# Instance normalisation of 65,536 rows: a direct emission of the program, and tiles whose rows are shared out in sixteen runs

## The chip, the cores and the metric

The kernel runs on one core of a Trainium2 chip. The metric is the device time of one execution in microseconds; lower is better. Several runs of the same program are taken, and their median is compared. A profile is one further execution, recorded by the hardware profiler.

## The reference

```python
def setup_inputs():
    batch = 256
    channels = 256
    length = 4096
    return {
        "x": np.random.randn(batch, channels, length).astype(np.float32),
        "eps": np.float32(1e-5),
    }

def reference(x, eps):
    mean = np.mean(x, axis=2, keepdims=True)
    var = np.var(x, axis=2, keepdims=True)
    return ((x - mean) / np.sqrt(var + eps)).astype(np.float32)
```

Each of the 256 x 256 = 65,536 rows of 4096 fp32 numbers is normalised by its own mean and variance. Rows do not depend on one another, so the order in which they are taken is free, as long as a result goes back to the place that its row came from. Input and output are 1.07 GB each, and every byte crosses the core once in each direction.

## The kernel before, in words

The rows are cut into 128 tiles of 512 rows. A tile lies in SBUF as 128 partitions (P) times K = 4 rows times 4096 numbers: 64 KB in a partition, 8 MB in all. In HBM a tile is one contiguous piece of 8 MB, and partition p holds the four rows that start at 64 KB times p. There are three tile buffers, `X[0]` to `X[2]` (BUFS = 3), and tile t uses buffer t mod 3.

Every wait is written out by hand with semaphores. The helper `take` waits for a count and clears the semaphore (L67 and L68). Four engines have work:

- SP issues every DMA. `load` (L170) waits until the buffer's last store has landed and then loads a tile; `store` (L165) waits until the tile's results are complete and writes it back. In the steady loop SP alternates: store tile t, then load tile t + 2 into the buffer that tile t - 1 left. `store_half` (L181) and two half loads (L199) handle the first and the last tile in halves, so that less lies bare at both ends.
- VectorE, in `vector_tile`, multiplies each row by 1/d and sums it in the same pass to get the mean (L87), forms the reciprocal of the deviation and the bias (L98, L100), and applies scale and bias to three and a quarter of the four rows (L112).
- ScalarE, in `scalar_tile`, squares and sums each row about its mean (L137), takes the square root (L146), and normalises the first 3072 numbers of the fourth row (L151).
- `rows_of` gives the piece of HBM for a tile. For a tile inside the loop the tile number comes from the loop's register.

The loop has 41 rounds of three tiles, tiles 2 to 124. Tiles 0 and 1 come ahead of it, and 125 to 127 after it. The program of each engine is written in a function of its own inside an `nc.Block()`.

A transfer of a tile is one DMA of 128 partitions. Sixteen DMA engines carry it out together, and each adds one to the transfer's semaphore when its share is through, so the wait is for 16.

Of the kernel before, what the change touches and what calls it, by code (L numbers as in the profile page):

```python
# [10 lines left out]
def kernel(  # L11
# [6 lines left out]
    nc = tc.nc  # L18
# [4 lines left out]
    P = 128  # L23
    K = 4
    BUFS = 3
    Q = 3072

    x_flat = x.flatten_outer_dims()
    out_flat = out.flatten_outer_dims()
    n, d = x_flat.shape  # L30
    assert n % (P * K) == 0 and d & (d - 1) == 0

    ntiles = n // (P * K)
    x_t = x_flat.rearrange("(t p k) d -> t p k d", p=P, k=K)
    out_t = out_flat.rearrange("(t p k) d -> t p k d", p=P, k=K)
    assert ntiles == 128

    half = K // 2

# [4 lines left out]
    eps_tile = pool.tile([P, 1], fp32)  # L44

    junk = psum.tile([P, d], fp32)
    X = [pool.tile([P, K, d], fp32, name=f"x{s}") for s in range(BUFS)]
# [8 lines left out]
    loaded = [nc.alloc_semaphore(f"loaded{s}") for s in range(BUFS + 1)]  # L56
    stored = [nc.alloc_semaphore(f"stored{s}") for s in range(BUFS + 1)]
# [6 lines left out]
    ready = nc.alloc_semaphore("ready")  # L64

    def take(engine, sem, count):
        engine.wait_ge(sem, count)  # L67
        engine.sem_clear(sem)  # L68

    V, A, S = nc.vector, nc.scalar, nc.sync  # L70

    def vector_tile(s, r0=0, k=K, ld=None, dn=None):

        x = X[s]
        ld = loaded[s] if ld is None else ld
        dn = done[s] if dn is None else dn
        own = 0

        def mine(instruction):
            nonlocal own  # L80
            own += 1
            return instruction.then_inc(own_v, 1)

        if ld:
            take(V, ld, 16)
        for r in range(r0, r0 + k):
            V.tensor_scalar(  # L87
                out=x[:, r, :], in0=x[:, r, :], scalar1=1.0 / d, scalar2=None, op0=ALU.mult, op1=ALU.add,
                accum_out=mean[s][:, r : r + 1],
            ).then_inc(means, 1)  # L90
        for b in range(r0, r0 + k, 2):
            c = slice(b, b + 2)
            final = b == r0 + k - 2
            if final:
                take(V, stds, (b - r0) // 2 + 1)
            else:
                V.wait_ge(stds, (b - r0) // 2 + 1)
            mine(V.reciprocal(out=rstd[s][:, c], in_=std[s][:, c]))  # L98
            V.wait_ge(own_v, own)
            mine(V.scalar_tensor_tensor(  # L100
                out=nbias[s][:, c], in0=mean[s][:, c], scalar=-1.0 / d, in1=rstd[s][:, c], op0=ALU.mult, op1=ALU.mult
            ))
            if final:
                take(V, own_v, own)
            else:
                V.wait_ge(own_v, own)
            if final:
                V.sem_inc(scaled, 1)
            for r in range(b, b + 2):
                c = slice(r, r + 1)  # L110
                f = slice(Q, d) if r == r0 + k - 1 else slice(0, d)
                V.tensor_scalar(  # L112
                    out=x[:, r, f], in0=x[:, r, f], scalar1=rstd[s][:, c], scalar2=nbias[s][:, c],
                    op0=ALU.mult, op1=ALU.add,
                ).then_inc(dn, 1)

    def scalar_tile(s, r0=0, k=K, ld=None, dn=None):

        x = X[s]
        dn = done[s] if dn is None else dn  # L120
        last = r0 + k - 1
        own = 0

        def mine(instruction):
            nonlocal own
            own += 1
            return instruction.then_inc(own_a, 1)

        for r in range(r0, last + 1):
            c = slice(r, r + 1)  # L130
            if own:
                A.wait_ge(own_a, own)
            if r == last:
                take(A, means, k)
            else:
                A.wait_ge(means, r - r0 + 1)
            mine(A.activation(  # L137
                out=junk, in_=x[:, r, :], func=AF.Square, bias=mean[s][:, c], scale=-float(d), accum_out=ss[s][:, c]
            ))
            if (r - r0) % 2:  # L140
                c = slice(r - 1, r + 1)
                if r == last:
                    take(A, own_a, own)
                else:
                    A.wait_ge(own_a, own)
                A.activation(  # L146
                    out=std[s][:, c], in_=ss[s][:, c], func=AF.Sqrt, bias=eps_tile, scale=1.0 / d**3
                ).then_inc(stds, 1)
        c = slice(last, last + 1)
        take(A, scaled, 1)  # L150
        A.activation(  # L151
            out=x[:, last, :Q], in_=x[:, last, :Q], func=AF.Identity, bias=nbias[s][:, c], scale=rstd[s][:, c]
        ).then_inc(dn, 1)

    def rows_of(ap, t):

        if isinstance(t, int):
            return ap[t]
        first, period, count, i = t
        ap = ap[first : first + period * (count - 1) + 1 : period]  # L160
        return ap[bass.ds(i, 1)].rearrange("o p k d -> p (o k) d")

    def store(s, t):
        take(S, done[s], K + 1)
        S.dma_start(out=rows_of(out_t, t), in_=X[s][:, :, :]).then_inc(stored[s], 16)  # L165

    def load(s, t, wait=True):
        if wait:
            take(S, stored[s], 16)
        S.dma_start(out=X[s][:, :, :], in_=rows_of(x_t, t)).then_inc(loaded[s], 16)  # L170

    def half_of(h):
        return slice(h * half, (h + 1) * half)

    def second(sems, s, h):
        return sems[BUFS] if h else sems[s]

    def store_half(s, t, h):
        r = half_of(h)
        take(S, second(done, s, h), half + 1)  # L180
        S.dma_start(out=out_t[t][:, r, :], in_=X[s][:, r, :]).then_inc(second(stored, s, h), 16)  # L181

    def halves(tile_fn, s, first):
        for h in range(2):
            ld = second(loaded, s, h) if first or h == 0 else False
            tile_fn(s, h * half, half, ld, second(done, s, h))

    last = ntiles - 1
    rounds = (ntiles - 5) // BUFS
    L0 = 2  # L190

    with tc.tile_critical():  # L192
        with nc.Block() as block:  # L193

            @block.sync
            def _(sync):
                for h in range(2):
                    r = half_of(h)
                    S.dma_start(out=X[0][:, r, :], in_=x_t[0][:, r, :]).then_inc(second(loaded, 0, h), 16)  # L199
                load(1, 1, wait=False)  # L200
                store_half(0, 0, 0)
                store_half(0, 0, 1)
                load(2, 2, wait=False)
                store(1, 1)
                take(S, stored[BUFS], 16)
                load(0, 3)

                with S.Fori(0, rounds) as i:
                    for t in range(L0, L0 + BUFS):
                        store(t % BUFS, (t, BUFS, rounds, i))  # L210
                        load((t + 2) % BUFS, (t + 2, BUFS, rounds, i))
                load(last % BUFS, last)
                store((last - 2) % BUFS, last - 2)
                store((last - 1) % BUFS, last - 1)
                store_half(last % BUFS, last, 0)
                store_half(last % BUFS, last, 1)
                for s in ((last - 2) % BUFS, (last - 1) % BUFS, last % BUFS, BUFS):
                    take(S, stored[s], 16)

            @block.vector  # L220
            def _(vector):
                V.memset(eps_tile, eps / d**2).then_inc(ready, 1)  # L222
                halves(vector_tile, 0, True)
                vector_tile(1)
                with V.Fori(0, rounds) as i:  # L225
                    for j in range(BUFS):
                        vector_tile((L0 + j) % BUFS)
                vector_tile((last - 2) % BUFS)
                vector_tile((last - 1) % BUFS)
                halves(vector_tile, last % BUFS, False)  # L230

            @block.scalar
            def _(scalar):
                take(A, ready, 1)
                halves(scalar_tile, 0, True)
                scalar_tile(1)
                with A.Fori(0, rounds) as i:
                    for j in range(BUFS):
                        scalar_tile((L0 + j) % BUFS)
                scalar_tile((last - 2) % BUFS)  # L240
                scalar_tile((last - 1) % BUFS)
                halves(scalar_tile, last % BUFS, False)


# [33 lines left out]
```

## Time and profile before

| What | Value |
|---|---|
| median of 9 runs | 4962.34 us (4961.73 to 4964.0) |
| the profiled execution, its own time | 4962.7 us |
| its span, first to last instruction | 4960.9 us |
| HBM read, written | 1073.74 MB each, 433 GB/s over the span |
| VectorE, ScalarE busy | 3297.8 us, 2407.6 us |
| transfers | 129 loads, 130 stores |
| a load or a store, time for SP to issue it (median) | 0.35 us, 0.34 us |
| from issue to landing (median) | loads 50.3 us, stores 31.5 us |

The times of one execution hang together as follows: the span is what the trace covers, and the execution's own time is some 2 us longer. The page's line of GB/s gives, for 40 equal slices of the span, what the core's DMA engines moved in both directions together. The time from issue to landing is long because a transfer queues behind those issued before it.

### The profile page before, as it was taken

The page shows a single profiled execution, that of the slowest core. Times are in us where ns is not written, and L with a number is a line of the kernel's source. Part 1 is how long each engine was busy: PE and PEld are TensorE (multiplying, and loading weights), DVE is VectorE, ACT ScalarE, POOL GpSimd, SP SyncE. Part 2 cuts the span into 40 slices and gives each one's busy share as a digit, 9 for nine tenths or more (in the row PEclk, how much of TensorE's full clock was granted, in tenths as well). Part 3 has the DMA queues.
Part 4 walks back from the last instruction along what each step waited for, and adds up shares of the span by engine and source line. Part 5 has one row for each costly group of instructions (what it writes and reads, how often), then busy time and mean ns, then how long its engine had stood idle before and what let it go on. Part 6 is the DMA issues. An engine that isn't in the chain of part 4 may idle for free.

```text
span 4960.9 us, 5954 instructions
## 1 busy us (share of the span) xinstructions
DVE 3297.8 (66%) x2049; ACT 2407.6 (49%) x1412; POOL 0.2 (0%) x4
## 2 busy tenths in 40 slices
DVE  6666666666666666666666666666666666666666
ACT  4445444554445544455445544455444554445544
POOL 0000000000000000000000000000000000000000
DMA  9999999999999999999999999999999999999999
GB/s 423 431 431 434 434 432 434 435 432 434 435 433 434 434 435 434 433 435 435 432 434 436 432 435 434 435 433 434 435 433 434 434 435 432 434 435 433 434 435 403
DMA packets 37298, 2147.52 MB, mean 433 GB/s; under 512 B 4144, under 2 KB 4144, under 8 KB 4144
## 3 DMA queue, kind: packets, MB, share of 16 engines
q1 hardware_dynamic: 37296, 2147.50, 100.0%
q14 instruction: 2, 0.02, 0.0%
HBM read 1073.74 MB, written 1073.74 MB: 433 GB/s over the span
## 4 chain that ended last, share of the span: by engine, by line
DVE 62%; another core or an unknown queue 31%; issue 4%; DMA 2%; ACT 0%; DVEq 0%; ACTq 0%; SPq 0%
DVE x L87 44%; DVE x L112 16%; DMA x<-in_x_dram 1%; DVE nbias L100 1%; DMA out_dram<-x 1%; DVE rstd L98 1%; ACT junk L137 0%; DVEq L68 0%; DVEq L225 0%; ACT L146 0%; ACT std L146 0%; DVEq L193 0%; ACTq L68 0%; ACTq L67 0%
## 5 line engine op out<-in xcount | busy, mean ns | idle before, releaser
L87 DVE TENSOR_SCALAR_CACHE_REDUCE x<-x 128x4096 f32<-128x4096 f32 x512 | 2232.3, 4416 | 1581.0 <-DMA x<-in_x_dram 1581.0
L137 ACT ACTIVATE junk<-x,mean 128x4096 f32<-128x4096 f32 x512 | 1883.1, 3678 | 2367.8 <-DVE x L87 2367.8
L112 DVE TENSOR_SCALAR x<-x,rstd,nbias 128x4096 f32<-128x4096 f32 (+1 forms) x512 | 1004.1, 2003 | 33.9 <-DVE nbias L100 29.2
L151 ACT ACTIVATE x<-x,nbias,rstd 128x3072 f32<-128x3072 f32 x130 | 383.2, 2947 | 146.0 <-DVEq L68 146.0
L137 ACT ACTIVATION_READ_ACCUMULATOR junk<-x,mean 128x1 f32 x512 | 95.5, 186 | 0.0
L146 ACT ACTIVATE std<-ss,eps_tile 128x2 f32<-128x2 f32 x256 | 75.6, 295 | 19.1
L98 DVE RECIPROCAL rstd<-std 128x2 f32<-128x2 f32 x256 | 40.6, 158 | 19.4 <-ACT std L146 19.4
L100 DVE SCALAR_TENSOR_TENSOR nbias<-mean,rstd 128x2 f32<-128x2 f32 x256 | 41.1, 160 | 8.9
L87 DVE DVE_READ_ACCUMULATOR x<-x 128x1 f32 x512 | 42.3, 83 | 0.0
L137 ACT ACT_TABLE_LOAD x1 | 1.3, 1283 | 1.2 <-DVE eps_tile L222 1.2
L146 ACT ACT_TABLE_LOAD x1 | 1.3, 1283 | 0.1
L222 DVE MEMSET eps_tile<- 128x1 f32 x1 | 0.1, 59 | 1.0 <-SPq L192 1.0
L259 POOL MEMSET const-uint8-127<- 128x1 uint8 x1 | 0.1, 102 | 0.0
L259 POOL MEMSET const-bfloat16-1.0<- 128x1 bf16 x1 | 0.1, 101 | 0.0
L259 POOL MEMSET const-float32-0.0<- 128x1 f32 x1 | 0.1, 98 | 0.2 <-issue 0.2
L259 POOL MEMSET const-float32-1.0<- 128x1 f32 x1 | 0.1, 98 | 0.0
## 6 DMA issues: line engine op xcount, KB each, us to landing
out_dram<-x SPq DMA_DIRECT2D x4, 4096.0 KB, 19.5
x<-in_x_dram SPq DMA_DIRECT2D x2, 4096.0 KB, 16.8
x<-in_x_dram SPq DMA_DIRECT2D x127, 50.3
out_dram<-x SPq DMA_DIRECT2D x126, 31.5
```

The costliest lines, as they stand in the source:

```text
L87: V.tensor_scalar(out=x[:, r, :], in0=x[:, r, :], scalar1=1.0 / d, scalar2=None, op0=ALU.mult, op1=ALU.add, accum_out=mean[s][:, r : r + 1 ...
L98: mine(V.reciprocal(out=rstd[s][:, c], in_=std[s][:, c]))
L100: mine(V.scalar_tensor_tensor(out=nbias[s][:, c], in0=mean[s][:, c], scalar=-1.0 / d, in1=rstd[s][:, c], op0=ALU.mult, op1=ALU.mult))
L112: V.tensor_scalar(out=x[:, r, f], in0=x[:, r, f], scalar1=rstd[s][:, c], scalar2=nbias[s][:, c], op0=ALU.mult, op1=ALU.add,).then_inc(dn, 1)
L137: mine(A.activation(out=junk, in_=x[:, r, :], func=AF.Square, bias=mean[s][:, c], scale=-float(d), accum_out=ss[s][:, c]))
L146: A.activation(out=std[s][:, c], in_=ss[s][:, c], func=AF.Sqrt, bias=eps_tile, scale=1.0 / d**3).then_inc(stds, 1)
L151: A.activation(out=x[:, last, :Q], in_=x[:, last, :Q], func=AF.Identity, bias=nbias[s][:, c], scale=rstd[s][:, c]).then_inc(dn, 1)
L222: V.memset(eps_tile, eps / d**2).then_inc(ready, 1)
L259: nc = _bacc.Bacc("TRN2", target_bir_lowering=False, num_devices=1)
```

## The change

Two things are changed. First, the instructions of the three engines are no longer emitted inside a block with a function per engine, but one after the other directly in the critical section. Second, the assignment of rows to tiles is different. The first two tiles (L0 = 128 mod 3 = 2) are contiguous as before. The other 126 tiles form 42 groups of three. A group is 24 MB of consecutive rows, cut in sixteen runs of 1.5 MB; each run is cut in three pieces of 512 KB, one for each tile of the group. A tile so consists of sixteen pieces of 512 KB that stand 1.5 MB apart, and piece e fills partitions 8e to 8e + 7. A partition still holds four consecutive rows of 64 KB in all. Loads and stores use the same assignment.

On the HBM side the access pattern of a transfer was 128 steps of 64 KB; for tiles 2 to 127 it is now 16 steps of 1.5 MB by 8 steps of 64 KB. On the SBUF side it is 128 partitions of 64 KB in both kernels. The order of instructions on each engine, their waits and their shapes are otherwise the same.

```diff
     ntiles = n // (P * K)
-    x_t = x_flat.rearrange("(t p k) d -> t p k d", p=P, k=K)
-    out_t = out_flat.rearrange("(t p k) d -> t p k d", p=P, k=K)
     assert ntiles == 128
+
+
+    E = 16
+    L0 = ntiles % BUFS
+
+    def by_tiles(ap):
+        groups = ap[L0 * P * K :].rearrange("(i e s j k) d -> s i e j k d", e=E, s=BUFS, k=K, j=P // E)
+        rest = ap[: L0 * P * K].rearrange("(t e j k) d -> t e j k d", e=E, k=K, j=P // E)
+        return groups, rest
+
+    x_t, out_t = by_tiles(x_flat), by_tiles(out_flat)
...
-    def rows_of(ap, t):
-
+    def rows_of(tiles, t):
+
+        groups, rest = tiles
         if isinstance(t, int):
-            return ap[t]
+            return rest[t] if t < L0 else groups[(t - L0) % BUFS][(t - L0) // BUFS]
         first, period, count, i = t
-        ap = ap[first : first + period * (count - 1) + 1 : period]
-        return ap[bass.ds(i, 1)].rearrange("o p k d -> p (o k) d")
+        assert period == BUFS
+        first -= L0
+        ap = groups[first % BUFS][first // BUFS : first // BUFS + count]
+        return ap[bass.ds(i, 1)].rearrange("o e j k d -> e (o j) k d")
...
-        S.dma_start(out=out_t[t][:, r, :], in_=X[s][:, r, :]).then_inc(second(stored, s, h), 16)
+        S.dma_start(out=rows_of(out_t, t)[:, :, r, :], in_=X[s][:, r, :]).then_inc(second(stored, s, h), 16)
...
-    L0 = 2
 
     with tc.tile_critical():
-        with nc.Block() as block:
-
-            @block.sync
-            def _(sync):
-                for h in range(2):
-                    r = half_of(h)
-                    S.dma_start(out=X[0][:, r, :], in_=x_t[0][:, r, :]).then_inc(second(loaded, 0, h), 16)
-                load(1, 1, wait=False)
...
+        for h in range(2):
+            r = half_of(h)
+            S.dma_start(out=X[0][:, r, :], in_=rows_of(x_t, 0)[:, :, r, :]).then_inc(second(loaded, 0, h), 16)
+        load(1, 1, wait=False)
...
```

More of the change, by code (lines that the diff above doesn't have):

```diff
@@ L189 @@
     rounds = (ntiles - 5) // BUFS
-    L0 = 2
     with tc.tile_critical():
-        with nc.Block() as block:
-            @block.sync
-            def _(sync):
-                for h in range(2):
-                    r = half_of(h)
-                    S.dma_start(out=X[0][:, r, :], in_=x_t[0][:, r, :]).then_inc(second(loaded, 0, h), 16)
-                load(1, 1, wait=False)
[L201 to L242, printed above, removed]
@@ new lines @@
+        for h in range(2):
+            r = half_of(h)
+            S.dma_start(out=X[0][:, r, :], in_=rows_of(x_t, 0)[:, :, r, :]).then_inc(second(loaded, 0, h), 16)
+        load(1, 1, wait=False)
+        store_half(0, 0, 0)
+        store_half(0, 0, 1)
+        load(2, 2, wait=False)
+        store(1, 1)
+        take(S, stored[BUFS], 16)
+        load(0, 3)
+        with S.Fori(0, rounds) as i:
+            for t in range(L0, L0 + BUFS):
+                store(t % BUFS, (t, BUFS, rounds, i))
+                load((t + 2) % BUFS, (t + 2, BUFS, rounds, i))
@@ new lines @@
+        load(last % BUFS, last)
+        store((last - 2) % BUFS, last - 2)
+        store((last - 1) % BUFS, last - 1)
+        store_half(last % BUFS, last, 0)
+        store_half(last % BUFS, last, 1)
+        for s in ((last - 2) % BUFS, (last - 1) % BUFS, last % BUFS, BUFS):
+            take(S, stored[s], 16)
+        V.memset(eps_tile, eps / d**2).then_inc(ready, 1)
+        halves(vector_tile, 0, True)
+        vector_tile(1)
+        with V.Fori(0, rounds) as i:
+            for j in range(BUFS):
+                vector_tile((L0 + j) % BUFS)
@@ L246 @@
+        vector_tile((last - 2) % BUFS)
+        vector_tile((last - 1) % BUFS)
+        halves(vector_tile, last % BUFS, False)
+        take(A, ready, 1)
+        halves(scalar_tile, 0, True)
+        scalar_tile(1)
+        with A.Fori(0, rounds) as i:
+            for j in range(BUFS):
+                scalar_tile((L0 + j) % BUFS)
+        scalar_tile((last - 2) % BUFS)
+        scalar_tile((last - 1) % BUFS)
+        halves(scalar_tile, last % BUFS, False)
 _INS = ['x', 'eps']
```

## The prediction

> **What bounds the kernel now.** I read the page first: its DMA slices, then the queue table.
>
> ```profile
> span 4960.9 us, 5954 instructions
> DVE 3297.8 (66%) x2049; ACT 2407.6 (49%) x1412; POOL 0.2 (0%) x4
> DMA  9999999999999999999999999999999999999999
> GB/s 423 431 431 434 434 432 434 435 432 434 435 433 434 434 435 434 433 435 435 432 434 436 432 435 434 435 433 434 435 433 434 434 435 432 434 435 433 434 435 403
> ...
> q1 hardware_dynamic: 37296, 2147.50, 100.0%
> ```
>
> VectorE is busy two thirds of the time and ScalarE half; the DMA engines are busy in every slice, and their packets fill 100.0% of sixteen engines' span. The trace's records of single packets sharpen this: a full row of a partition is one packet of 65,536 B, and the 1st, 50th and 95th percentile of its duration are all 2.418 us. The first packet starts some 2 us into the span and the last ends some 2 us before its end; between lie 4957.1 us, and the packets' durations sum to 4957.6 us per engine. Nothing is idle. Each engine moves 2147.48 MB / 16 / 65,536 B = 2048 such packets, 2048 x 2.418 = 4952.1 us. So all that a better pattern of addresses could win is 4957.6 - 4952.1 = 5.5 us, 0.11% of the span.
>
> Where those 5.5 us are: the second and third slices show 431 GB/s, most later ones 434. The trace also keeps the sixteen increments of each transfer's semaphore, one per DMA engine. Their spread is 0.5 to 0.7 us for the first seven transfers, grows by about 0.5 us with most loads (stores add nothing) to 4.5 us at 524 us, is 5.5 us from 795 us on, and then hardly moves for 2900 us. Engines which start in step lose time against each other while they load, and drift apart until they no longer meet.
>
> Then the waits, of the engines and of the DMA queue on SP:
>
> ```profile
> ACT junk L137 <- DVE x L87: 2367.8, 512, 18.2
> DVE x L87 <- DMA x<-in_x_dram: 1581.0, 126, 13.6
> ```
>
> ```profile
> SPq L68 <- DVE x L112: 4757.4, 130, 38.4
> ```
>
> VectorE waits for a load before 126 tiles, 12.5 us each; SP waits for VectorE, but that costs nothing while the rings hold work. How much they hold is in the timeline of two tiles at mid-run:
>
> ```profile
> 2433.60 0.34 SPq L165 DMA_DIRECT2D out_dram<-x  x1
> 2434.18 0.35 SPq L170 DMA_DIRECT2D x<-in_x_dram  x1
> 2445.80 4.42 DVE L87 TENSOR_SCALAR_CACHE_REDUCE x<-x 128x4096 f32<-128x4096 f32 x1 [12.44 <-DMA x<-in_x_dram]
> ...
> 2472.10 0.34 SPq L165 DMA_DIRECT2D out_dram<-x  x1
> 2472.68 0.35 SPq L170 DMA_DIRECT2D x<-in_x_dram  x1
> 2484.45 4.42 DVE L87 TENSOR_SCALAR_CACHE_REDUCE x<-x 128x4096 f32<-128x4096 f32 x1 [12.57 <-DMA x<-in_x_dram]
> ```
>
> A tile takes 2484.45 - 2445.80 = 38.65 us, which is 16 packets of 2.418 us (8 of the load, 8 of the store). When a load has landed, a store and a load are queued behind it (38.7 us); the next issue comes 26.3 us later. The slack is 12 us for the engine that lands last.
>
> [...]65,536 B / 2.418 us = 27.1 GB/s per engine, and the first, load-only transfers run at that rate from their second packet[...].
>
> **The change, part by part.** The direct emission removes a few branches at the head and the end of each engine's program. Before, SP issues its first load 0.96 us into the span. I book -0.5 us; the bounds are 0 and -1. Arithmetic, waits and their order stay the same on VectorE, ScalarE and SP, instruction by instruction, and so do the bytes and the 128 rows of 64 KB per transfer.
>
> The DRAM side of a transfer changes. From tile 2 on its pattern is 16 runs (1.5 MB apart) x 8 partitions x 64 KB; it no longer merges to 128 equal steps. Tiles 0 and 1 keep the merged form. 126 loads and 126 stores (two of these in halves) are affected.
>
> (a) Issue. SP needs 0.34 us for a transfer. If three dimensions double that, the store comes 0.34 and the load 0.7 us later, under the 12 us slack: nothing, and under 1 us a tile if the cover were gone (126 us at most).
>
> (b) HBM addresses. [...]Gain: at most the 4.8 us of slow packets after the start.[...] I take 0.
>
> (c) Which engine takes which partition. [...]From below: nothing[...]. From above: half rate throughout, 252 transfers x 8 packets x 2.418 us = 4875 us.
>
> Between these ends stands whether a pair stays in step. With the two a time s apart, four packets (9.67 us) overlap only for 9.67 - s, so the extra cost of a tile is 4 x (9.67 - s).[...] In the trace of before, engines that met did drift apart, always in the same sense[...]. I therefore take it that pairs separate here too. If they take m tiles, with s growing evenly, the cost is m x 4 x 9.67 / 2 = m x 19.3 us. For m from 1 to 20 (the spread before took about 20 loads) that is 19 to 387 us; I take m = 4, 77 us. The late partner's 9.67 us are in it, and show up in the tail. Afterwards it costs nothing, just: an early engine runs out 38.7 - 9.67 = 29.0 us after its partner's landing, and new work arrives 26.3 us + about 1.1 us (from the first issue to the first packet) after it; 1.6 us are left.
>
> Sum, against the profiled execution's own 4962.7 us (span 4960.9; median of nine 4962.34): 4962.7 - 0.5 + 77 = 5039, say 5040 us.
>
> **Rivals.**
> - Lockstep. [...]Before, the spread stood still at 0.6 us over the first seven transfers, so nothing drifts of itself. The waits make it worse: a pair that gets ahead runs dry, then both start together on the next issue. With s about 1 us, the extra is 126 x 4 x 8.7 = 4385, 9350 us in all; fully locked 9837; with s at 5 us, as before's spread, 7300. Against it: engines under contention did separate.
> - No contention (not slower). [...]What remains is -0.5 us and between 0 and -4.8 us of (b): 4957 to 4962, about 4960.[...]
> - Partly separated: some pairs stay together for part of the run, 5400 to 7300 us.
> - Faster by over 0.2%: needs 9.9 us, and only 6 are there.
>
> **How the numbers follow.** Pairs separate 0.40 (own range 4980 to 5400 us), lockstep 0.33 (7300 to 9837), no contention 0.20, partly 0.05, faster 0.02. The time is that of the first, 5040 us. From 4957 to 9400 us lie the first, the third, the fourth and over half of the second, about 0.8 in all. Changes of up to 0.2% either way (9.9 us) are what a measurement here can't tell from none: faster 0.02, same 0.20, slower 0.78.
>
> **What would show it.** Contention: 64 KB packets of up to 4.84 us right after tile 2's load, against 2.42 before, and GB/s in the second slice well under 431. Separation: these long packets die out and later slices are back at 434, a tile at 38.65 us, with a spread of landings near 10 us. Lockstep: slices at 220 to 290 to the end, waits of VectorE for loads of some 45 us a tile, span twofold. No contention: slices 434 from the second on, tile period unchanged. (a) is right if the issue rows stay far below 12 us. My prediction is wrong if no packet beyond the first tiles lasts over 3.5 us, or if packets stay long to the end.

## The result, and the profile after

The changed kernel takes 9053.51 us (median of 10 runs, 8921.93 to 9117.91) where before takes 4962.75 us in the same comparison: 1.8139 times as long, 95% interval 1.8104 to 1.8174. The ratio is taken over the five fast runs of the changed kernel (8921.93 to 9044.78 us); its other five lie over 1.5% above the fastest. Its profiled execution took 9039.64 us, with a span of 9037.9 us. That is neither the forecast 5040 us nor its mechanism; it is close to the lockstep rival, 9350 us.

From the page of the changed kernel, the same lines as those of before:

```profile
span 9037.9 us, 5938 instructions
DVE 3297.9 (36%) x2049; ACT 2407.7 (27%) x1412; POOL 0.2 (0%) x4
...
DMA  9999999999999999999999999999999999999998
GB/s 290 247 245 235 235 240 239 238 238 236 238 239 239 236 236 238 238 236 235 235 236 243 248 234 237 238 236 237 233 232 234 235 235 234 233 233 233 235 234 212
...
q1 hardware_dynamic: 37296, 2147.50, 99.6%
```

VectorE and ScalarE do the same work in the same time. The DMA engines are still busy throughout and carry the same 37,296 packets, but move 232 to 248 GB/s in place of some 434, from the second slice to the last but one. A busy share of 99.6% says here that each packet takes longer, not that more is moved.

The waits of the engines and of SP's queue (who waited for whom, us in total, times, longest):

```profile
ACT junk L146 <- DVE x L96: 6401.4, 512, 53.9
DVE x L96 <- DMA x<-in_x_dram: 5614.6, 127, 49.3
```

```profile
SPq L77 <- DVE x L121: 8029.1, 129, 66.5
SPq L77 <- DMA out_dram<-x: 799.5, 126, 70.7
```

VectorE's wait for loads has grown from 1581.0 to 5614.6 us, by 4034 us: nearly the whole loss. SP's second line has grown too: a load now waits for the store that frees its buffer at almost every tile, 6 us each. Before, there were three such waits:

```profile
SPq L68 <- DMA out_dram<-x: 47.7, 3, 30.7
```

Two tiles in the timeline at mid-run (start, us, engine, line, what):

```profile
4417.71 4.42 DVE L96 TENSOR_SCALAR_CACHE_REDUCE x<-x 128x4096 f32<-128x4096 f32 x1 [45.20 <-DMA x<-in_x_dram]
...
4444.01 0.60 SPq L177 DMA_DIRECT2D out_dram<-x  x1
4450.45 0.56 SPq L182 DMA_DIRECT2D x<-in_x_dram  x1
4488.10 4.42 DVE L96 TENSOR_SCALAR_CACHE_REDUCE x<-x 128x4096 f32<-128x4096 f32 x1 [44.31 <-DMA x<-in_x_dram]
```

A tile takes 70.4 us instead of 38.65. The trace's records of single packets show how: in tile 2's load, the first with the new pattern, every engine's 64 KB packets take 4.9 to 5.1 us from the second on, and the load takes 40 us. The store that follows is tile 1's, which still has 128 equal steps, and its packets are back at 2.42 us. Over the whole run 66% of the packets take over 4.5 us per 64 KB and 12% under 2.6; the rest lie between.

### The profile page after: what moved, and what is told of

Read it like the earlier page. It is cut to its first block, busy times and chain, and to the rows that moved or that the text cites. A ratio compares the mean times of both kernels' runs of the same rounds, so it can differ in the third digit from the quotient of the medians.

```text
span 9037.9 us, 5938 instructions
## 1 busy us (share of the span) xinstructions
DVE 3297.9 (36%) x2049; ACT 2407.7 (27%) x1412; POOL 0.2 (0%) x4
## 3 DMA queue, kind: packets, MB, share of 16 engines
q1 hardware_dynamic: 37296, 2147.50, 99.6%
## 4 chain that ended last, share of the span: by engine, by line
another core or an unknown queue 62%; DVE 35%; issue 2%; ACT 0%; DMA 0%; DVEq 0%; ACTq 0%; SPq 0%
DVE x L96 25%; DVE x L121 9%; DVE nbias L109 1%; DVE rstd L107 0%; ACT junk L146 0%; DMA x<-in_x_dram 0%; DVEq L77 0%; DVEq L230 0%; ACT std L155 0%; ACT L155 0%; ACTq L77 0%; ACTq L76 0%; SPq L276 0%; SPq L203 0%
## 5 line engine op out<-in xcount | busy, mean ns | idle before, releaser
L96 DVE TENSOR_SCALAR_CACHE_REDUCE x<-x 128x4096 f32<-128x4096 f32 x512 | 2232.3, 4416 | 5614.6 <-DMA x<-in_x_dram 5614.6
```

The lines of the kernel that those rows point to most:

```text
L96: V.tensor_scalar(out=x[:, r, :], in0=x[:, r, :], scalar1=1.0 / d, scalar2=None, op0=ALU.mult, op1=ALU.add, accum_out=mean[s][:, r : r + 1 ...
```

## The experiments

Three causes stood against each other. The first is the forecast's: two DMA engines of a transfer, a pair, hold each other up where the partitions that they serve bring them together, in blocks of four packets (9.67 us). Pairs and blocks are my assumption: no record names the engine or the partition of a packet. The expectations call this the port theory. The second is the addresses in HBM, the third a pattern of three dimensions being slow as such. A fourth question, the one that the prediction got wrong, was why engines that hold each other up don't come apart.

**The direct emission alone.** The changed kernel with contiguous tiles:

```diff
-        groups = ap[L0 * P * K :].rearrange("(i e s j k) d -> s i e j k d", ...)
+        groups = ap[L0 * P * K :].rearrange("(i s e j k) d -> s i e j k d", ...)
```

> The changed kernel with contiguous tiles, as before: only the direct emission is left of the change. Every theory of the 4091 us ([...]the addresses in HBM, the pattern that does not merge) expects the time of before here, 4962 us within 2 us, with a gain of 0 to 1 us from the branches. If it stays above 5000 us, the direct emission has a part in the loss.

Measured: 4962.0 us against 4962.51, ratio 1.0003 (0.9979 to 1.0026), span 4960.2 us. The direct emission has no part in the loss; a gain of half a microsecond can't be told from nothing.

**The same spread of rows, in equal steps.** Now a partition's 64 KB stand 192 KB after those of the partition before it, in the same groups of 24 MB:

```diff
-        groups = ap[L0 * P * K :].rearrange("(i e s j k) d -> s i e j k d", ...)
+        groups = ap[L0 * P * K :].rearrange("(i e j s k) d -> s i e j k d", ...)
```

> The rows of a tile lie as far apart as in the changed kernel (groups of 24 MB, eight partitions in every 1.5 MB), but one partition stands 192 KB after the other, so the pattern merges to 128 equal steps. Port theory (the loss comes from which engine serves which partitions): 4958 to 4968 us, packets of 64 KB at 2.42 us. HBM theory (tiles spread over 24 MB are slow to read and write): 8500 us or more. Pattern theory (three dimensions are slow): 4958 to 4968 us too.

Measured: 4962.88 us against 4962.51, ratio 1.0015 (0.9993 to 1.0038). Its span and GB/s on the page:

```profile
span 4961.1 us, 5938 instructions
...
GB/s 422 432 437 431 434 434 431 435 435 432 436 433 433 437 433 434 435 432 435 434 432 436 434 433 437 433 433 436 433 435 434 432 435 434 433 436 432 433 437 397
```

Every slice is at the rate of before. Tiles spread over 24 MB cost nothing.

**Contiguous tiles with a 16 x 8 pattern.** The reverse: a tile is one piece of 8 MB, but partition 8e + j takes its block 16j + e:

```diff
-        groups = ap[L0 * P * K :].rearrange("(i e s j k) d -> s i e j k d", ...)
+        groups = ap[L0 * P * K :].rearrange("(i s j e k) d -> s i e j k d", ...)
```

> Each tile is one contiguous piece of 8 MB again, but partition 8e + j takes its block 16j + e, so the pattern is 16 x 8 blocks and doesn't merge. Port theory: as slow as the changed kernel, 8500 to 9500 us[...]. HBM theory (1.5 MB between the engines is the cause): 4962 us to 5100 us. Pattern theory: about 9050 us.

Measured: 9049.33 us, ratio 1.8204 (1.8088 to 1.832), the loss of the changed kernel. With the pattern's sixteen runs starting 64 KB apart and not 1.5 MB, and the tile in one piece, it is all there. So the 1.5 MB between the runs in HBM fall as its cause. Left are the pairs and the pattern's third dimension.

**Pairs alone.** A kernel without computation, four transfers of each of four kinds, one at a time, loads into and then stores from one buffer:

```python
for n in range(4):      # (a)
    S.dma_start(out=B[0][0:32], in_=G[0][n][0:4]).then_inc(loaded[0], 16)
    wait_in()
...                     # (b) B[0][0:32] <- G[1][n][0:8, 0:4]
...                     # (c) B[0][0:64] <- G[0][n + 4][0:8]
...                     # (d) B[0][0:64] <- G[1][n + 4][0:16, 0:4]
```

> No computation: four kinds of transfer, each four times and each alone, loads first and then stores, all with three dimensions and runs 1.5 MB apart. (a) four engines, eight partitions each, partitions 0-31; (b) eight engines, four partitions each, partitions 0-31; (c) eight engines, eight partitions each, partitions 0-63; (d) sixteen engines, four partitions each, partitions 0-63. Port theory: (a) and (b)[...] packets of 2.42 us, landing after about 21 and 12 us; in (c)[...] packets of about 5.1 us, 42 us; in (d)[...] 22 us. Pattern theory and HBM theory: (a) and (c) alike, (b) and (d) alike.

The queue's issues in its timeline; from one line's start to the next are four transfers (L214 to L223 the loads a to d, L226 to L235 the stores):

```profile
22.93 66.84 SPq L214 DMA_DIRECT2D x<-in_x_dram  x4
111.01 37.64 SPq L217 DMA_DIRECT2D x<-in_x_dram  x4
160.25 128.91 SPq L220 DMA_DIRECT2D x<-in_x_dram  x4
331.19 68.23 SPq L223 DMA_DIRECT2D x<-in_x_dram  x4
421.60 65.28 SPq L226 DMA_DIRECT2D out_dram<-x  x4
507.78 35.09 SPq L229 DMA_DIRECT2D out_dram<-x  x4
553.67 126.96 SPq L232 DMA_DIRECT2D out_dram<-x  x4
722.13 66.58 SPq L235 DMA_DIRECT2D out_dram<-x  x4
```

One load takes 22.0, 12.3, 42.7 and 22.6 us; stores 21.5, 11.5, 42.1 and 22 us. The increments of the semaphores show that 4, 8, 8 and 16 engines carried them, as planned. (a) and (c) have the same pattern with eight packets per engine, and so have (b) and (d) with four; the time doubles from (a) to (c) and from (b) to (d), where partitions 32 to 63 are in the transfer beside 0 to 31. (b) and (c) both use eight engines, so it isn't their number. (c) and (d) move the same 4 MB to or from the same partitions, and (c), with half the engines, takes twice as long. In the packet records the median is 2.42 us in (a) and (b), and 5.0 to 5.1 us in (c) and (d), with no packet of (c) or (d) under 3.5 us: all their engines are slowed. Some 2.1 times the packet's time fits two engines that take turns; which two, and where they meet, the records don't show. What they show is that the partitions in the transfer separate slow from fast among these four kinds, in both directions, and that neither three dimensions nor runs 1.5 MB apart slow a packet by themselves.

**One direction at a time.** Only the loads, then only the stores, take the 16 x 8 pattern; the other side goes to contiguous tiles, and the rows come out in another order:

```diff
-    x_t, out_t = by_tiles(x_flat), by_tiles(out_flat)
+    x_t, out_t = by_tiles(x_flat, "i e s j k"), by_tiles(out_flat, "i s e j k")
...
```

This is the edit for the loads; for the stores the two strings change places.

> Loads take the changed kernel's rows (16 x 8 pattern), stores go to contiguous tiles with 128 equal steps; the rows come out in another order than the reference has. Port theory, engines staying in step: a load takes 8 x 5.1 = 41 us and a store 19.3, some 60 us a tile, 7300 to 7600 us.[...]

> The reverse: loads of contiguous tiles with 128 equal steps, stores with the changed kernel's 16 x 8 pattern; again the rows come out in another order. Port theory, engines in step: 19.3 us for a load and 32 to 41 for a store, 6600 to 7600 us.[...]

Measured: 7514.8 us for the loads (two runs, 7505.44 and 7524.16) and 6679.35 us for the stores (6628.86 and 6729.84), both within the ranges expected of engines in step. That is some 2550 us and some 1700 us above before. Loads cost more than stores, and the two add up to 4200 to 4300 us, near the 4091 of both together. Neither direction is free, and plain transfers between do not bring pairs apart for good.

**A stream without computation, and the same with the pairs set apart.** 40 loads and 40 stores of the changed kernel's pattern; the stores read a buffer that nothing writes. SP still waits, before each load and each store, until all sixteen engines have landed the one of its kind two earlier. The second kernel differs in two stores ahead, of 4 runs and of 12. They were meant to set some engines back by one block and some by two, so that the two of each pair start a block (9.67 us) apart; which engine was set back how far isn't shown.

```diff
+        S.dma_start(out=O[0][40][0:4, 0:4], in_=B[2][0:16]).then_inc(stored[2], 16)
+        S.dma_start(out=O[0][41][0:12, :, 0 : 2 * d], in_=B[2][0:96, 0 : 2 * d]).then_inc(stored[3], 16)
         for n in range(N):
```

> No computation and no wait of a store for results: 40 loads and 40 stores with the changed kernel's pattern, the stores from a buffer that nothing writes, so two to three transfers always stand in the rings. Separation (my prediction's step, with the waits of the full kernel to blame for its failure):[...] 1600 to 1900 us. Even-handed sharing[...]: nothing drifts, 40 x 70 to 82 = 2800 to 3300 us.

> As the stream before, but two extra stores ahead of it[...]. If a distance is kept once it is there: 64 KB packets at 2.42 us, 40 x 38.7 + 50 = about 1600 us. If [...]anything else pulls the engines together again: close to the stream's time without it.

Measured: 2907.67 us and 1615.46 us (one run each). Their spans and GB/s, the plain stream first:

```profile
span 2905.9 us, 208 instructions
...
GB/s 274 227 238 256 289 300 275 244 246 239 235 234 233 235 235 231 235 233 232 233 233 234 235 233 232 234 233 232 230 231 232 233 231 233 234 229 234 235 188 55
```

```profile
span 1613.7 us, 212 instructions
...
GB/s 342 379 400 426 434 427 437 437 429 437 434 437 430 435 435 430 439 432 437 429 435 437 427 437 437 429 437 434 437 430 435 439 427 439 434 435 432 435 434 210
```

The 80 transfers are the same; the two stores ahead of them make 1292 us of difference. From the fourth slice to the last but one the second stream lies at 426 to 439 GB/s, with the changed kernel's own pattern at its own distances in HBM. So the delay at the start is enough, and, to judge by the rate, engines once apart stay apart.

The plain stream takes the time expected of even-handed sharing, but its trace doesn't show that nothing drifts. The sixteen landings of a transfer lie within 0.8 us for the first load of the pattern and are spread over 46 us at 322 us, and in the sixth slice (363 to 436 us) the rate has risen to 300 GB/s. Then it falls back to 235. The packet records show what comes between. With sixteen packets under way at once, every one of the sixteen engines has work. From 458 to 467 us it is mostly 13 or 14, down to 12: the engines that are ahead have carried out all that SP had issued. SP issues the next store at 466.40 us, and four packets start almost at the same moment, at 467.63 to 467.76 us. So engines that get ahead run dry (nothing is queued for them), and the next issue starts them in step.

That still happens without computation, so this stream did not clear the full kernel's waits of the suspicion that they hold pairs together. Between 30% and 80% of the span, fewer than sixteen packets are under way for 3.9% of the time in the plain stream and for 2.7% in the changed kernel, but for 0.2% in the stream set apart and in the kernel before. The loads-only kernel shows another side. Its slices:

```profile
GB/s 324 281 290 297 291 286 285 292 289 285 284 284 292 287 286 283 284 289 285 284 282 281 284 286 285 284 281 281 285 286 286 283 280 283 288 285 285 282 279 280
```

From 1700 us on almost no engine runs dry there (0.1 to 0.3% of the time in each slice but the last), and yet the rate stays at 279 to 292 GB/s to the end. So, to judge by the rate, nothing drives the pairs apart in that kernel, where the loads alone have the slow pattern; and nothing drives those of the stream set apart together.

**Shorter blocks.** If the distance that a pair lacks is the length of a block (the four packets, 9.67 us, as assumed), shorter transfers need less of it. Loads and stores were cut in halves, with VectorE starting on the first half, then again with the distance set at the start:

```diff
-        S.dma_start(out=X[s][:, :, :], in_=rows_of(x_t, t)).then_inc(loaded[s], 16)
+        for h in range(2):
+            r = half_of(h)
+            S.dma_start(out=X[s][:, r, :], in_=half_rows(x_t, t, r)).then_inc((loaded_b if h else loaded)[s], 16)
```

```diff
+        for c, k in ((4, 0), (12, 1)):
+            S.dma_start(
+                out=rows_of(out_t, last)[:c, :, k, :], in_=X[0][: 8 * c, k, :]
+            ).then_inc(apart, 16)
         load(2, 2, wait=False)
```

> The changed kernel's rows and 16 x 8 pattern, with each load and store issued as two halves (32 KB a partition), and VectorE starting on the first half when that has landed. Blocks[...] are half as long, and the rings hold some 8 us more work when SP issues. Engines in step, the slowest pair setting the pace: still 8500 to 9300 us. If the long blocks or the short rings were what kept pairs together: under 6500 us.

> The same with one addition: ahead of tile 2's load two extra stores[...]. If only the missing distance within the pairs makes the changed kernel slow, and a distance is kept: 4970 to 5400 us, with most of the time at 434 GB/s[...]. If full-kernel waits pull the pairs together again: above 8000 us.

Measured: 5848.36 us (5739.85 and 5956.87) and 5529.51 us (5494.04 and 5564.97). The halves contradict the expectation of 8500 to 9300 us. Their slices:

```profile
GB/s 327 272 305 328 321 383 376 340 330 350 376 370 343 316 334 347 339 369 380 364 336 310 307 370 409 424 427 425 426 428 429 428 428 427 427 427 428 427 429 392
```

For 3300 us they wander between 270 and 385 GB/s; then, to judge by the rate, the pairs are apart and stay so. The run with the distance set:

```profile
GB/s 398 396 331 327 346 330 333 334 328 313 356 369 336 325 363 395 403 345 378 385 419 430 431 430 431 431 431 431 430 428 429 428 431 428 431 431 431 431 431 401
```

It began near 400 GB/s, lay between 313 and 403 from the third slice on (275 us), and was back at 430 near 2900 us. Its time lies in neither of the expected ranges. The set distance didn't last in the full kernel, and the packet records show when it went. From 80 to 340 us at most 2% of the packets take over 4.5 us per 64 KB. At 340.83 to 340.95 us four engines that had been without work for 2 to 4 us start together, 0.7 us after SP's issue, and from 340 to 400 us 21 to 69% of the packets take that long. The loss had begun before that, with more packets between 2.6 and 4.5 us and 340 to 391 GB/s from 280 to 340 us. This fits waits which pull engines together again; since no run changed the waits alone, it isn't shown as the cause.

Two things had changed in the halves, the block and VectorE's early start, which leaves more work in the rings. So halves once more, VectorE waiting for the whole tile, and quarters (one row of a partition per DMA, PARTS = 4) in the same manner:

```diff
+    PARTS = 2
...
+        for r in parts:
+            S.dma_start(out=X[s][:, r, :], in_=part_rows(x_t, t, r)).then_inc(loaded[s], 16)
```

> The changed kernel with every load and store issued as two halves, but VectorE waits for the whole tile, so the rings hold no more than in the changed kernel when SP issues. If the shorter block[...] let the halves kernel before come apart: again 5300 to 6500 us, with slices near 430 GB/s late in the run. If the earlier start of VectorE, hence fuller rings, did it: 8000 to 9300 us.

> The same with four DMAs per load and store, one row of each partition: blocks of 2.42 us. If the distance that a pair needs is the block's length, it is reached sooner than with halves: below 5500 us, most slices at 420 to 430 GB/s. If engines merely stay in step whatever the block: about 9000 us.

Measured: 6719.04 us (6615.4 and 6822.68), between the two ranges expected, and 5131.45 us, ratio 1.0339 (1.0289 to 1.0389). Halves first (the longer run), then quarters:

```profile
GB/s 316 290 321 339 328 327 322 315 320 344 313 300 309 309 301 303 310 305 299 308 314 281 299 333 336 305 318 315 356 305 310 338 314 302 299 308 346 318 324 294
```

```profile
GB/s 341 341 415 416 411 413 415 419 422 422 426 428 426 424 424 423 424 419 421 422 424 424 425 425 425 425 423 426 426 422 425 426 426 423 425 425 426 426 426 383
```

With blocks of 9.67, 4.84 and 2.42 us (four packets of 64, 32 and 16 KB) the kernel takes 9054, 6719 and 5131 us. Late halves never settle within their run; quarters do within 260 us. Both changes in the first halves kernel counted: shorter transfers alone take 9054 to 6719 us, the early start the rest to 5848; the two runs of the one don't overlap those of the other. The early start also leaves engines without work less often: fewer than sixteen packets are under way for 4.9% of the time between 30% and 80% of the span, for 14% without it. That it is the length of the block that counts, and not another effect of more and shorter transfers, is argued and not shown. Of the quarters' 168 us above before, some 53 are their smaller packets (2.444 us per 64 KB for 2.418, over 2048 packets per engine).

## Why the prediction was wrong

- What bounds before, and that at most 5.5 us could be won: nothing contradicts it. No pattern tried here was measurably faster than before, the equal steps included.
- Direct emission, booked -0.5 us: not distinguishable from nothing.
- (a) Issue: SP takes 0.56 to 0.60 us instead of 0.34 and 0.35, 0.2 to 0.3 us more per transfer. The doubling that I allowed for was on the high side. The stream set apart, whose transfers SP issues in the same 0.57 us, reaches full rate, which supports the zero.
- (b) HBM addresses, taken as 0: right, by the equal steps (4962.88 us), by the contiguous piece (9049.33 us) and by the stream set apart (the changed kernel's pattern at some 434 GB/s).
- (c) Which engine takes which partition: this was my assumption, and no record shows it. That a transfer of the new pattern can take twice as long was right: 42.7 us for (c) against 22.0 for (a). A packet that is held up is dearer than the doubled 4.84 us: 5.1.
- The step that failed is "I therefore take it that pairs separate here too", with "I take m = 4, 77 us". The cost measured is 4091 us, 32.5 us for each of 126 tiles: in mid-run a load's landing comes 38 us after the store's before it, and a store's 32 to 33 us after the load's, where both were 19.3. The long packets do not die out: they are 66% of all, over the whole run. Two parts of the step's reasoning failed.
  - "In the trace of before, engines that met did drift apart": that was no measure for the new pattern. The packets of before are at 2.418 us from the 1st to the 95th percentile, so its engines lose little against each other, and where they lose it isn't shown. In (c) and (d) of the pairs kernel no packet is under 3.5 us: all their engines are slowed, and none comes through at its old rate. In the loads-only kernel the rate stays at 279 to 292 GB/s from 1700 us to the end, at 7503 us. The prediction also had both figures to compare, a drift that ended at 5.5 us and the 9.67 us that its pairs need.
  - "Afterwards it costs nothing, just", with 1.6 us left: here an engine that gets ahead was taken to have work always. The landings of the changed kernel spread over 0.9 us at tile 2's load and over 42 us at 420 us, so its engines do drift, and much further than a block. But from 400 to 413 us only 11 to 15 packets are under way, SP issues at 412.13 us, and four engines start together, at 413.39 to 413.58 us.

  How much of the 4091 us belongs to each of the two stays open.
- The lockstep rival had the right time for partly the right reason, and with some luck. Its "a pair that gets ahead runs dry, then both start together on the next issue" is close to what the traces show, for single engines. But engines were not all in step: the sixteen increments of one transfer are spread over some 40 us in mid-run, and a third of the packets is not long. Its price was too low, which hides this: with 5.1 us for 4.84, full lockstep would cost 252 x 8 x 2.68 = some 5400 us (an estimate) and not 4875. Each wait is for all sixteen, so engines that get ahead gain nothing for the kernel. That the slowest pair alone sets the pace fits this; the packet records name no engine, so it is argued and not shown, and so is which two of the engines that start together make a pair.
- No contention, the rival on the other side, fell at the pairs kernel.

The tell-tales named in advance worked: packets of over 4.84 us in tile 2's load, a second slice far below 431, and long packets to the end.

## What to carry to other kernels

Before changing the HBM side of a full-speed DMA, time the new pattern in a kernel without computation: here 128 equal steps kept the packets of 64 KB at 2.42 us, 16 x 8 brought two thirds of them over 4.5 us, and the kernel took 1.81 times as long. If rows must be spread, spread them in equal steps from partition to partition, which cost nothing in these runs (4962.88 us against 4962.51). And when a stall is expected to dissolve because workers drift apart, ask what drives them apart, and follow the one that gets ahead: in these traces it ran out of work, and the next issue started it together with others. A distance set on purpose lasted in the stream where engines hardly ran dry (0.2% of the time), and was lost in the halves kernel within 60 us of such a start.

## What was unexpected

Where engines hold each other up, a packet of 64 KB takes 5.1 us, not 2 x 2.418 = 4.84: the doubling and another 5%. And a whole stream of the same transfers ran at some 233 or 434 GB/s, depending on two smaller stores ahead of it. Nor did the engines of the slow pattern stay in line: in the plain stream they spread over 46 us within eight transfers, and it was a wait meant for buffers that put some of them back in step.
